# Finishing the last 128 output rows in two column pieces, with two loads and six subtractions on other engines

## The chip, the core and the metric

The kernel runs on one core of a Trainium2 chip. The core has a matmul engine (TensorE, PE in the profile; its weight loads have a row of their own, PEld), and VectorE (DVE), ScalarE (ACT), GpSimd (POOL) and SyncE (SP), which issues most of the DMAs. Each engine works through its own list of instructions in order and waits at semaphores for the others. The metric is the time of one execution on the device in microseconds; less is better. The runs of the kernel before took 843.01, 843.52 and 845.77 us, median 843.52.

## The reference

One inference step of a two-layer trunk for a prompt of 512 rows and a sample group of 8 x 4 = 32 rows, all in float32, width 1024. The first layer is a pooling mixer with memory attention; the second is multi-head latent attention (8 heads, rotary part of 64, a paged cache of 4096 positions for the sample group) with memory attention. What the change touches is the end of the second layer:

```
# second layer
mixed = concat([tok * silu(gate_t), mem_o * silu(gate_m)], -1)   # 1536 wide
x = x + mixed @ w_out[l]                                          # 1536 x 1024
...
# the end: for each row
y = x * rsqrt(mean(x * x) + 1e-6) * g_final
```

and, in the attention, the tables of the rotary part:

```
rope(x) = concat([x1 * cos - x2 * sin, x1 * sin + x2 * cos])
```

## The kernel before, in words

Matmuls run on numbers that are split in two: `split` (lines 88 to 91) makes a high part by a cast on ScalarE and a low part by a subtraction on VectorE or GpSimd, and `mm3` (lines 93 to 96) issues three matmuls, high by high, high by low and low by high, into the same sum. So each weight tile costs a load, a cast, a subtraction, and each product three matmuls.

The program goes through the first layer, the second layer's projections and its memory attention, and then comes to a stretch in which the order on PE and on SP is written out by the program itself (`manual_schedule`, lines 918 to 921). There, `weave` (line 933) takes generators, each a thread of work (`round_scores`, `round_values` for the sample group's cache pages, `gates_late`, `head_inputs`, `heads` for the prompt's attention, `out_all` for the output product, `sample_out` for the sample rows' end), and always lets the one that is furthest behind issue its next piece; a generator yields the time that its piece is planned to take and the time until its next piece may start. The order on ScalarE, VectorE and GpSimd, including the DMAs that GpSimd issues, is chosen by the framework's scheduler from a simulated timeline.

The places that matter here:

- Lines 1138 to 1149: the pools of the heads' stage take over the space of the projections' weights; the two rotary tables, `tab`, are loaded there by SP, 128 x 512 numbers each (256 KB), ahead of the rest of the cache pages that SP loads (line 985). GpSimd issues the loads of the heads' weights (`load_q`, `load_pair`, lines 1151 to 1164). `rope_T` (lines 739 to 749), with GpSimd as its engine, is the tables' reader. The `tab` buffers are used again for two parts of the product's input (`mix_b`, line 1308).
- `prepare` (line 1329): for one slab of the output weights (two blocks of 128 rows by 512 columns, 512 KB) it loads it by SP (`slab`, line 1322), casts the high part on ScalarE and has GpSimd subtract the low part. There are six slabs for each of two column halves, `fh` 0 and 1, so twelve; three buffers each. For the first half it also splits the parts of the product's input that the slab needs (`mix_b`).
- `out_rows` (line 1356): the product for one column half, as four blocks `j` of 128 rows by 512 columns, each in one accumulation bank of the tag "oa". For slab after slab, each block gets 2 x 3 matmuls; the slabs 4 and 5 are done together at the end (the list `late`), so that a block's last 12 matmuls stand together and it is finished before the next block's begin.
- `done` (line 1366): the end of a block. VectorE adds the residual (line 1369), ScalarE squares and sums along the row (line 1370). In the second half, VectorE adds the two halves' sums (line 1375), `rstd_cols` (line 153) has VectorE divide by the width and add the epsilon (line 155) and GpSimd take the power of -0.5 (line 159), ScalarE scales the first column half (line 1379), VectorE scales the second and multiplies it by the gain (line 1381), and SP stores each half (lines 1380 and 1382).
- `sample_out` (line 1558): the sample rows' output product, its two sums in banks of the tag "ac" (line 1570), of which there are two (line 959).

Of the kernel before, what the change touches and what calls it, by code (L numbers as in the profile page):

```python
# [8 lines left out]
F32R = mybir.dt.float32r  # L9
U32 = mybir.dt.uint32  # L10
I32 = mybir.dt.int32
AF = mybir.ActivationFunctionType
ALU = mybir.AluOpType
AX = mybir.AxisListType

P = 128
D = 1024
KD = 8
SEQ = 512
# [5 lines left out]
EPS = 1e-6  # L25
# [13 lines left out]
def trunk_kernel(ctx: ExitStack, tc: tile.TileContext, A, O):  # L39
    nc = tc.nc  # L40
# [35 lines left out]
    def fr(ap):  # L76
        return ap.bitcast(F32)
# [10 lines left out]
    def split(h, l, src, eng=None):  # L88
        nc.scalar.copy(h, src)  # L89
        (eng or nc.vector).tensor_tensor(out=l, in0=src, in1=fr(h), op=ALU.subtract)  # L90
        return h, l

    def mm3(out, wh, wl, xh, xl, start, stop):
        nc.tensor.matmul(out, lhsT=wh, rhs=xh, start=start, stop=False)  # L94
        nc.tensor.matmul(out, lhsT=wh, rhs=xl, start=False, stop=False)  # L95
        nc.tensor.matmul(out, lhsT=wl, rhs=xh, start=False, stop=stop)  # L96
# [16 lines left out]
    ps_ = Banks(pa=4, tr=3, ac=1)  # L113

    def cst(shape, dt=F32):
        return const.tile(shape, dt, name=nm("c"))

    def st(n):
        return small("s", n=n)
# [11 lines left out]
    mhalf = cst([P, 16])  # L131
# [18 lines left out]
    def gain(base, k):  # L150
        return gT[:, base + k : base + k + 1]

    def rstd_cols(ssq, n, rows, width, r=None):
        v = st(n)
        nc.vector.tensor_scalar(
            out=v[:rows], in0=ssq[:rows], scalar1=1.0 / width, scalar2=EPS, op0=ALU.mult, op1=ALU.add
        )
        r = st(n) if r is None else r
        nc.gpsimd.tensor_tensor(out=r[:rows], in0=v[:rows], in1=mhalf[:rows, :n], op=ALU.pow)
        return r  # L160
# [45 lines left out]
    def load_w(src, k, c):  # L206
        t = pw("wr")
        v = t[:, : k * c].rearrange("p (k c) -> p k c", k=k)
        nc.sync.dma_start(v, src)
        return t, v  # L210

    def split_w(t, k, c, eng=None):
        n = k * c
        h, l = split(pw("wh", F32R, n), pw("wl", F32R, n), t[:, :n], eng)
        return h.rearrange("p (k c) -> p k c", k=k), l.rearrange("p (k c) -> p k c", k=k)
# [289 lines left out]
    for k in range(KD):  # L505
        for i in range(2):
            wh, wl = (t.rearrange("p (k c) -> p k c", k=KD) for t in fw[i])
            for half in range(2):
                o = half * HALF
                h, l = hx[k]  # L510
# [10 lines left out]
    t, v = load_w(wa[22], KD, P)  # L521
    wh, wl = split_w(t, KD, P)
# [118 lines left out]
    for f in range(KD):  # L641
        pts = [ps_("pa"), ps_("pa")]
        for s in range(2):
            t = pw("wr")
            nc.sync.dma_start(t[:, :768], wo[f, s].rearrange("p k c -> p (k c)"))
            wh, wl = split_w(t, 6, P, nc.gpsimd)
            for half in range(2):
                o = half * HALF
                for i, k in enumerate(order[s * 6 : s * 6 + 6]):
                    h, l = mixed[k]  # L650
# [26 lines left out]
    for f in (2, 0, 1):  # L677
        c = P if f < 2 else 64
        t, v = load_w(wkv[:, f * P : f * P + c].rearrange("(k p) c -> p k c", p=P), KD, c)
        if f < 2:  # L680
            wh, wl = split_w(t, KD, c)
# [28 lines left out]
    for j in range(4):  # L710
        t = xo("o")
        for k0 in range(0, KD, 4):
            ps = ps_("tr")
# [5 lines left out]
    ps = ps_("tr")  # L719
# [14 lines left out]
    for f in range(2):  # L734
        nc.vector.scalar_tensor_tensor(
            out=ck[f], in0=ck[f], scalar=gain(G_CKV, f), in1=rc, op0=ALU.mult, op1=ALU.mult
# [15 lines left out]
    tab = [rp("c"), rp("c")]  # L752
# [7 lines left out]
    ps = ps_("tr")  # L760
# [201 lines left out]
    def ps_(tag):  # L962
        return (rb if tag in rb.tags else hb)(tag)
# [180 lines left out]
    def pat(tag, dt=F32, n=None):  # L1144
        return next(p for p in (heads_raw, heads_val, heads_in) if tag in p.tags)(tag, dt, n)

    tab = [pat("tab"), pat("tab")]
    nc.sync.dma_start(tab[0], A["c_cos"][:, :SEQ])
    nc.sync.dma_start(tab[1], A["c_sin"][:, :SEQ])

    def load_pair(n):
        t = pat("wu")
# [152 lines left out]
    fin = Pool("fin", "left", wr=(D, 3), wh=(D, 3), wl=(D, 3))  # L1305
    mixed = {}

    def mix_b(k):
        if k >= 8:
            t = pat("tab")  # L1310
            nc.gpsimd.dma_start(t, gmd[k - 8])
            mixed[k] = split(pc("c", F32R), pat("p", F32R), t)
        else:
            mixed[k] = split(pc("c", F32R), (pg("g", F32R) if k else pt("t", F32R))[:, :SEQ], gt[k][:, :SEQ])

    wo = A["w_out_b"]
    ssq = st(8)
    sss = st(2)
    slabs = [(fh, s) for fh in range(2) for s in range(6)]
    order = ([0, 1], [2, 3], [4, 5], [8, 9], [10, 11], [6, 7])  # L1320
# [1 line left out]
    def slab(t, fh, s):  # L1322
        k = order[s][0]
        v = t.rearrange("p (k c) -> p k c", k=2)
        src = wo[k * P : (k + 2) * P, fh * 512 : (fh + 1) * 512]
        nc.sync.dma_start(v, src.rearrange("(k p) c -> p k c", p=P))
        return v

    def prepare(fh, s):
        if fh == 0:  # L1330
            for k in order[s]:
                mix_b(k)
        t = fin("wr")
        slab(t, fh, s)
        wh, wl = split(fin("wh", F32R), fin("wl", F32R), t, nc.gpsimd)
        return wh.rearrange("p (k c) -> p k c", k=2), wl.rearrange("p (k c) -> p k c", k=2)

    prepared = [prepare(*slabs.pop(0)) for _ in range(3)]
    x1n, gains_f = [], []

# [14 lines left out]

    def out_rows(fh):
        pts = [ps_("oa") for _ in range(4)]
        pts = [pts[j] for j in (0, 3, 1, 2)]

        def run(s, j, wh, wl):  # L1360
            c = slice(j * P, (j + 1) * P)
            for i, k in enumerate(order[s]):
                h, l = mixed[k]
                mm3(pts[j], h[:, c], l[:, c], wh[:, i, :], wl[:, i, :], s == 0 and i == 0, s == 5 and i == 1)

        def done(j):
            f = slice(fh * 512, (fh + 1) * 512)
            xf = x1n[j][:, f]
            nc.vector.tensor_tensor(out=xf, in0=pts[j], in1=xf, op=ALU.add)
            nc.scalar.activation(pat("wu"), xf, AF.Square, accum_out=ssq[:, 2 * j + fh : 2 * j + fh + 1])  # L1370
            if fh == 0:
                nc.vector.tensor_tensor(out=xf, in0=xf, in1=gains_f[0][:, f], op=ALU.mult)
                return
            sq = st(1)
            nc.vector.tensor_tensor(
                out=sq, in0=ssq[:, 2 * j : 2 * j + 1], in1=ssq[:, 2 * j + 1 : 2 * j + 2], op=ALU.add
            )
            r = rstd_cols(sq, 1, P, D)
            nc.scalar.activation(x1n[j][:, :512], x1n[j][:, :512], AF.Copy, scale=r)
            nc.sync.dma_start(O["y_p"][0, j * P : (j + 1) * P, :512], x1n[j][:, :512])  # L1380
            nc.vector.scalar_tensor_tensor(out=xf, in0=xf, scalar=r, in1=gains_f[0][:, f], op0=ALU.mult, op1=ALU.mult)
            nc.sync.dma_start(O["y_p"][0, j * P : (j + 1) * P, 512:], xf)

        late = []
        for s in range(6):
            wh, wl = prepared.pop(0)
            late.append((s, wh, wl))
            if s == 4:
                continue
            for j in range(4):  # L1390
                for one in late:
                    run(one[0], j, *one[1:])
                    yield 1.4, 0.0
                if s == 5:
                    if not x1n:
                        yield lambda: x1n
                    done(j)
            for _ in late:
                if slabs:
                    prepared.append(prepare(*slabs.pop(0)))  # L1400
            late = []

    def out_all():
        yield from out_rows(0)
        yield from out_rows(1)
# [35 lines left out]
    out = Thread(out_all(), 112 / total, 66 / total, 66.0, now[0])  # L1441
# [293 lines left out]
```

## Time and profile before

| what | us |
|---|---|
| runs: median (lowest, highest) | 843.52 (843.01, 845.77) |
| the profiled execution's own time | 836.92 |
| its span in the profile | 835.2 |
| PE busy in the span | 792.8 |
| VectorE, ScalarE, GpSimd busy | 506.1, 326.9, 262.4 |

The page of the profile gives the busy time of each engine, the span in forty slices, the DMA queues, the chain of work that ended last, and the costliest groups of instructions. A row of a group names the line, the engine, the operation, the tile written and the tiles read, their shapes and the count; then the busy time in microseconds, the mean of one in nanoseconds, and the idle time of the engine just before such instructions with what ended it. A row of the timeline begins with the start and the duration in microseconds; a bracket at its end is the idle time before it and the releaser. A row of a window gives its length and then the busy time and count of PE, PEld, DVE, ACT and POOL, the granted clock of PE, the DMA share and GB/s. In the list of waits each row says who waited for whom, the total, how often, and the longest. A wait is put down to what came last by the profile. Matmuls are pipelined: a row's duration runs into the next one's, so the distance between starts is what a matmul costs in a stream.

The profiled execution was 836.92 us long, 6.60 us under the median of the runs; 1.7 us of it lie around the span.

### The profile page before, as it was taken

The numbers are of one execution on the slowest core, as the hardware profiler recorded it, in microseconds if no ns is written. First come the engines' busy times: TensorE is split into PE (matmuls) and PEld (weight loads), VectorE is DVE, ScalarE is ACT, GpSimd is POOL, SyncE is SP. The second block draws the span as 40 slices with busy tenths as digits, with TensorE's granted clock in tenths as the row PEclk, the third lists the DMA queues.
The fourth block names the chain that finished last, engine by engine and source line by source line (L and its number), as shares of the span: only waits on it lengthen the run. The fifth ranks groups of instructions, "written<-read, shape, count | busy, mean of one in ns | idle before, by whom it ended". The sixth has DMA issues, their size and how long they took to land.

```text
span 835.2 us, 17542 instructions
## 1 busy us (share of the span) xinstructions
PE 792.8 (95%) x6906; PEld 680.8 (82%) x6906; DVE 506.1 (61%) x941; ACT 326.9 (39%) x650; POOL 262.4 (31%) x213
## 2 busy tenths in 40 slices
PE   6999999978999999999999999899999999999995
PEld 6989998978999989877999897776767767677674
DVE  6757666888763435775766653665665577643313
ACT  7453333322343226335433323444543545342212
POOL 0035223434334313411522342642250230055321
PEclk9999999999999999999999999999999999999999
DMA  8356246511233234636625785967978767776642
GB/s 302 98 179 225 76 177 228 158 58 52 68 121 96 77 120 150 206 89 221 227 89 183 260 295 181 366 225 239 300 246 279 262 205 247 261 267 236 215 177 107
DMA packets 82100, 158.01 MB, mean 189 GB/s; under 512 B 9185, under 2 KB 34402, under 8 KB 81762
## 3 DMA queue, kind: packets, MB, share of 16 engines
q1 hardware_dynamic: 77170, 141.22, 50.9%
q0 software_dynamic: 4848, 15.67, 5.2%
q8 instruction: 54, 0.88, 0.4%
q14 instruction: 28, 0.23, 0.1%
HBM read 147.23 MB, written 9.64 MB: 188 GB/s over the span
## 4 chain that ended last, share of the span: by engine, by line
PE 73%; DVE 10%; DMA 8%; issue 3%; ACT 3%; POOL 2%; SPq 1%; POOLq 0%; DVEq 0%; ACTq 0%
PE pa L94 14%; PE pa L96 14%; PE pa L95 14%; PE tr L135 5%; PE ac L1028 3%; PE ac L1067 3%; DVE v L583 2%; DMA o<-ostore 2%; PE oa L94 2%; PE oa L95 2%; DMA b<-in_cache_P 2%; PE oa L96 2%; PE ac L1039 1%; PE ac L389 1%; SPq L985 1%
## 5 line engine op out<-in xcount | busy, mean ns | idle before, releaser
L94 PE MATMUL pa<-h,wh 128*128 128x272 f32 x832 | 239.7, 291 | 4.5 <-DVE g L613 4.5
L96 PE MATMUL pa<-h,wl 128*128 128x272 f32 x832 | 236.9, 290 | 0.6 <-POOL wl L90 0.6
L90 POOL TENSOR_TENSOR wl<-wr,wh 128x1024 fp32r<-128x1024 f32 (+1 forms) x67 | 156.0, 2330 | 234.7 <-ACT wh L89 220.6
L95 PE MATMUL pa<-h,wh 128*128 128x272 f32 x640 | 184.3, 289 | 0.0
L94 PEld LDWEIGHTS pa<-h,wh 128*128 128x128 f32 x832 | 156.9, 189 | 9.3 <-issue 5.8
L96 PEld LDWEIGHTS pa<-h,wl 128*128 128x128 f32 x832 | 155.6, 189 | 2.4 <-POOL wl L90 1.5
L89 ACT CAST wh<-wr 128x1024 fp32r<-128x1024 f32 (+1 forms) x87 | 87.7, 1008 | 168.4 <-issue 66.8
L95 PEld LDWEIGHTS pa<-h,wh 128*128 128x128 f32 x640 | 120.9, 189 | 1.0
L261 DVE SCALAR_TENSOR_TENSOR g<-t,g 128x272 f32<-128x272 f32 x48 | 49.5, 1037 | 15.3 <-ACT t L260 15.3
L95 PE MATMUL pa<-g,wh 128*128 128x272 f32 x192 | 54.5, 288 | 0.1
L260 ACT ACTIVATE t<-g 128x272 f32<-128x272 f32 x48 | 20.3, 428 | 78.6 <-DVE g L247 78.0
L135 PE MATMUL tr<-c,b 128*128 128x128 f32 x256 | 40.0, 277 | 3.0 <-DVE kt L996 1.7
L94 PE MATMUL oa<-wh,c 128*128 128x512 f32 x96 | 39.5, 412 | 0.0
L95 PE MATMUL oa<-wl,c 128*128 128x512 f32 x96 | 38.0, 395 | 0.7 <-POOL wl L90 0.7
L135 PEld LDWEIGHTS tr<-c,b 128*128 128x128 f32 x256 | 29.7, 140 | 9.7 <-issue 3.0
L95 PEld LDWEIGHTS pa<-g,wh 128*128 128x128 f32 x192 | 36.1, 188 | 0.3 <-DVE g L90 0.3
L994 ACT COPY kt<-tr 128x512 f32<-128x512 f32 x43 | 25.3, 589 | 27.0 <-PE tr L135 26.0
L247 DVE SCALAR_TENSOR_TENSOR g<-pa,r 128x272 f32<-128x272 f32 x42 | 18.2, 438 | 28.8 <-PE pa L96 28.8
L1028 PE MATMUL ac<-kt,c 128*32 128x256 f32 x256 | 35.0, 393 | 0.0
L1028 PE MATMUL ac<-a,c 128*32 128x256 f32 x256 | 34.7, 392 | 0.0
L90 DVE TENSOR_TENSOR q<-q,q 128x512 fp32r<-128x512 f32 x16 | 27.2, 1700 | 10.0 <-ACT q L89 9.9
L90 DVE TENSOR_TENSOR wl<-wr,wh 128x1024 fp32r<-128x1024 f32 x20 | 24.5, 1224 | 12.3 <-ACT wh L89 12.2
(380 smaller groups left out, 1813.0 us busy)
## 6 DMA issues: line engine op xcount, KB each, us to landing
a<-in_cache_P SPq DMA_DIRECT2D x128, 288.0 KB, 4.7
b<-in_cache_P SPq DMA_DIRECT2D x128, 160.0 KB, 4.9
wr<-in_w_in_a SPq DMA_DIRECT2D x24, 512.0 KB, 3.6
wr<-in_w_in_b SPq DMA_DIRECT2D x19, 512.0 KB, 3.6
cs<-in_mem_kT SPq DMA_DIRECT2D x16, 512.0 KB, 5.7
wr<-in_w_out_a SPq DMA_DIRECT2D x16, 384.0 KB, 3.1
wr<-in_w_out_b SPq DMA_DIRECT2D x12, 512.0 KB, 6.3
ws<-in_w_out_b SPq DMA_DIRECT2D x12, 512.0 KB, 5.6
```

Of the source, the lines that this page charges most:

```text
L89: nc.scalar.copy(h, src)
L90: (eng or nc.vector).tensor_tensor(out=l, in0=src, in1=fr(h), op=ALU.subtract)
L94: nc.tensor.matmul(out, lhsT=wh, rhs=xh, start=start, stop=False)
L95: nc.tensor.matmul(out, lhsT=wh, rhs=xl, start=False, stop=False)
L96: nc.tensor.matmul(out, lhsT=wl, rhs=xh, start=False, stop=stop)
L135: nc.tensor.transpose(out, in_, ident[:k, :k])
L247: nc.vector.scalar_tensor_tensor(out=out[:, o : o + HALF], in0=ps[:, :HALF], scalar=scale, in1=bc[:, o : o + HALF], op0=ALU.mult, op1=ALU. ...
L260: nc.scalar.activation(th[:, :HALF], z[:, o : o + HALF], AF.Tanh)
L261: nc.vector.scalar_tensor_tensor(out=z[:, o : o + HALF], in0=th[:, :HALF], scalar=1.0, in1=z[:, o : o + HALF], op0=ALU.add, op1=ALU.mult,)
L994: nc.scalar.copy(out, src)
L1028: nc.tensor.matmul(o[j * NS : (j + 1) * NS, :], lhsT=QT[:, k, b, :], rhs=(nat[ih][0][:, :, PGW + k * P : PGW + (k + 1) * P] if j < 2 else ...
L1067: nc.tensor.matmul(po[j * NS : (j + 1) * NS, :256], lhsT=pT[:, i * P + j * NS : i * P + (j + 1) * NS], rhs=nat[i // 2][j // 2][:, j % 2 * ...
```

## The change

Three edits. The two rotary tables are loaded by GpSimd's queue instead of SP's. The six slabs of the first column half have their low part subtracted by VectorE, those of the second half by GpSimd as before. And in the second column half the last block (block 3, rows 384 to 511) is summed in two pieces of 256 columns, the first in its "oa" bank, the second in an "ac" bank; each is added to the residual and squared by itself. The row sum is put together otherwise for all blocks: the square takes the factor 1024^-0.5 with it, so the sum is a mean already; the epsilon and the sums that are known earlier are added ahead, and behind the last square stand one addition on VectorE and the power on GpSimd.

```
-    nc.sync.dma_start(tab[0], A["c_cos"][:, :SEQ])
-    nc.sync.dma_start(tab[1], A["c_sin"][:, :SEQ])
+    nc.gpsimd.dma_start(tab[0], A["c_cos"][:, :SEQ])
+    nc.gpsimd.dma_start(tab[1], A["c_sin"][:, :SEQ])
...
-    ssq = st(8)
+    ssq = st(16)
...
-        wh, wl = split(fin("wh", F32R), fin("wl", F32R), t, nc.gpsimd)
+        wh, wl = split(fin("wh", F32R), fin("wl", F32R), t, nc.vector if fh == 0 else nc.gpsimd)
...
+        pieces = [[(pts[j], 0, 512)] for j in (0, 3, 1, 2)]
+        if fh:
+            pieces[3] = [(pts[2], 0, 256), (ps_("ac"), 256, 256)]
+
+        def run(s, j, piece, wh, wl):
+            ps, o, n = piece
+            c, w = slice(j * P, (j + 1) * P), slice(o, o + n)
             for i, k in enumerate(order[s]):
                 h, l = mixed[k]
-                mm3(pts[j], h[:, c], l[:, c], wh[:, i, :], wl[:, i, :], s == 0 and i == 0, s == 5 and i == 1)
+                mm3(ps[:, :n], h[:, c], l[:, c], wh[:, i, w], wl[:, i, w], s == 0 and i == 0, s == 5 and i == 1)
+        def done(j, p, ps, o, n):
+            f = slice(fh * 512 + o, fh * 512 + o + n)
             xf = x1n[j][:, f]
-            nc.vector.tensor_tensor(out=xf, in0=pts[j], in1=xf, op=ALU.add)
-            nc.scalar.activation(pat("wu"), xf, AF.Square, accum_out=ssq[:, 2 * j + fh : 2 * j + fh + 1])
+            nc.vector.tensor_tensor(out=xf, in0=ps[:, :n], in1=xf, op=ALU.add)
+            c = 4 * j + 2 * fh + p
+            nc.scalar.activation(pat("wu", n=n), xf, AF.Square, scale=D ** -0.5, accum_out=ssq[:, c : c + 1])
...
+            if p < len(pieces[j]) - 1:
+                return
+            others = [4 * j] + [4 * j + 2 + i for i in range(p)]
+            so_far = EPS
+            for i, o_ in enumerate(others):
+                nc.vector.tensor_scalar(
+                    out=sm[:, i : i + 1], in0=ssq[:, o_ : o_ + 1], scalar1=so_far, scalar2=None, op0=ALU.add
+                )
+                so_far = sm[:, i : i + 1]
+            r = st(1)
+            nc.vector.tensor_scalar(
+                out=sm[:, 2:3], in0=ssq[:, c : c + 1], scalar1=so_far, scalar2=None, op0=ALU.add
             )
-            r = rstd_cols(sq, 1, P, D)
+            nc.gpsimd.tensor_tensor(out=r, in0=sm[:, 2:3], in1=mhalf[:, :1], op=ALU.pow)
             nc.scalar.activation(x1n[j][:, :512], x1n[j][:, :512], AF.Copy, scale=r)
...
             for j in range(4):
-                for one in late:
-                    run(one[0], j, *one[1:])
-                    yield 1.4, 0.0
+                for p, piece in enumerate(pieces[j]):
+                    for one in late:
+                        run(one[0], j, piece, *one[1:])
+                        yield 1.4 / len(pieces[j]), 0.0
```

More of the change, by code (lines that the diff above doesn't have):

```diff
@@ L1357, in out_rows @@
         pts = [ps_("oa") for _ in range(4)]
-        pts = [pts[j] for j in (0, 3, 1, 2)]
-        def run(s, j, wh, wl):
-            c = slice(j * P, (j + 1) * P)
+        pieces = [[(pts[j], 0, 512)] for j in (0, 3, 1, 2)]
[4 more added lines that the diff above has]
+            c, w = slice(j * P, (j + 1) * P), slice(o, o + n)
             for i, k in enumerate(order[s]):
                 h, l = mixed[k]
-                mm3(pts[j], h[:, c], l[:, c], wh[:, i, :], wl[:, i, :], s == 0 and i == 0, s == 5 and i == 1)
-        def done(j):
-            f = slice(fh * 512, (fh + 1) * 512)
+                mm3(ps[:, :n], h[:, c], l[:, c], wh[:, i, w], wl[:, i, w], s == 0 and i == 0, s == 5 and i == 1)
+        def done(j, p, ps, o, n):
+            f = slice(fh * 512 + o, fh * 512 + o + n)
             xf = x1n[j][:, f]
-            nc.vector.tensor_tensor(out=xf, in0=pts[j], in1=xf, op=ALU.add)
-            nc.scalar.activation(pat("wu"), xf, AF.Square, accum_out=ssq[:, 2 * j + fh : 2 * j + fh + 1])
+            nc.vector.tensor_tensor(out=xf, in0=ps[:, :n], in1=xf, op=ALU.add)
+            c = 4 * j + 2 * fh + p
+            nc.scalar.activation(pat("wu", n=n), xf, AF.Square, scale=D ** -0.5, accum_out=ssq[:, c : c + 1])
             if fh == 0:
@@ L1373, in done @@
                 return
-            sq = st(1)
-            nc.vector.tensor_tensor(
-                out=sq, in0=ssq[:, 2 * j : 2 * j + 1], in1=ssq[:, 2 * j + 1 : 2 * j + 2], op=ALU.add
+            sm = st(3)
+            if p < len(pieces[j]) - 1:
[10 more added lines that the diff above has]
+                out=sm[:, 2:3], in0=ssq[:, c : c + 1], scalar1=so_far, scalar2=None, op0=ALU.add
             )
-            r = rstd_cols(sq, 1, P, D)
+            nc.gpsimd.tensor_tensor(out=r, in0=sm[:, 2:3], in1=mhalf[:, :1], op=ALU.pow)
             nc.scalar.activation(x1n[j][:, :512], x1n[j][:, :512], AF.Copy, scale=r)
             nc.sync.dma_start(O["y_p"][0, j * P : (j + 1) * P, :512], x1n[j][:, :512])
-            nc.vector.scalar_tensor_tensor(out=xf, in0=xf, scalar=r, in1=gains_f[0][:, f], op0=ALU.mult, op1=ALU.mult)
+            xf = x1n[j][:, 512:]
+            nc.vector.scalar_tensor_tensor(out=xf, in0=xf, scalar=r, in1=gains_f[0][:, 512:], op0=ALU.mult, op1=ALU.mult)
             nc.sync.dma_start(O["y_p"][0, j * P : (j + 1) * P, 512:], xf)
@@ L1390, in out_rows @@
             for j in range(4):
-                for one in late:
-                    run(one[0], j, *one[1:])
-                    yield 1.4, 0.0
[L1394 to L1397, printed above, removed]
+                for p, piece in enumerate(pieces[j]):
+                    for one in late:
+                        run(one[0], j, piece, *one[1:])
+                        yield 1.4 / len(pieces[j]), 0.0
+                    if s == 5:
+                        if not x1n:
+                            yield lambda: x1n
+                        done(j, p, *piece)
             for _ in late:
```

## The prediction

> **What bounds the kernel now.** I read the page first, then who waited for whom on the matmul engine in the last stage, then that stage in order of time.
>
> ```profile
> span 835.2 us, 17542 instructions
> PE 792.8 (95%) x6906; PEld 680.8 (82%) x6906; DVE 506.1 (61%) x941; ACT 326.9 (39%) x650; POOL 262.4 (31%) x213
> ```
> ```profile
> PE tr L1509 <- DMA o<-ostore: 1.1, 1, 1.1
> PE tr L135 <- ACT rt L1050: 1.1, 1, 1.1
> PE oa L95 <- POOL wl L90: 0.7, 1, 0.7
> PE ac L1575 <- DMA ws<-in_w_out_b: 0.4, 1, 0.4
> ```
> ```profile
> 505.00:724.00 219.00, 208.86 (x2248) 156.85 (x2247) 138.88 (x314) 100.93 (x240) 63.51 (x65) 1.00 0.76 251
> ```
> The matmul engine (PE) works 95% of the span. From 724 us on it waits only four times, 3.3 us together (second fence, the window from 724 to 836 us), and one of the four, 0.7 us, is for a low part made by GpSimd: this is what the second part of the change touches. The third fence is one long window in the attention stage before it, its length and then PE's busy time; I come back to it under C. The last matmul ends at 826.54 us (its row stands below), and 8.7 us pass from there to the end of the span: this tail is what the first part of the change touches. So there are two places with something to win, and both are small.
>
> **The first weights' low parts.** This is the spot where PE goes from the last head to the output product.
>
> ```profile
> 736.49 1.05 ACT L89 CAST wh<-wr 128x1024 fp32r<-128x1024 f32 x1 [0.85 <-DMA wr<-in_w_out_b]
> 737.66 0.27 ACT L89 CAST p<-hs 128x128 fp32r<-128x128 f32 x1
> 737.82 1.05 ACT L89 CAST wh<-wr 128x1024 fp32r<-128x1024 f32 x1
> ```
> ```profile
> 737.67 5.18 POOL L90 TENSOR_TENSOR wl<-wr,wh 128x1024 fp32r<-128x1024 f32 x2 [14.57 <-ACT wh L89]
> ```
> ```profile
> 737.96 0.29 DVE L90 TENSOR_TENSOR p<-hs,p 128x128 fp32r<-128x128 f32 x1 [3.87 <-ACT p L89]
> 738.17 0.68 DVE L996 COPY kt<-tr 128x512 f32<-128x512 f32 x1
> 738.76 4.64 DVE L90 TENSOR_TENSOR p<-tab,c 128x512 fp32r<-128x512 f32 x2
> ```
> ```profile
> 738.86 0.28 PE L102 MATMUL po<-p,vx 128*128 128x128 f32 x1
> 738.97 0.45 PE L94 MATMUL oa<-wh,c 128*128 128x512 f32 x1
> 740.10 0.50 PE L95 MATMUL oa<-wl,c 128*128 128x512 f32 x1 [0.68 <-POOL wl L90]
> ```
> ```profile
> L90 DVE TENSOR_TENSOR wl<-wr,wh 128x1024 fp32r<-128x1024 f32 x20 | 24.5, 1224 | 12.3 <-ACT wh L89 12.2
> L90 DVE TENSOR_TENSOR g<-g,c 128x512 fp32r<-128x512 f32 x7 | 4.8, 686 | 0.2
> ```
> ScalarE casts the first slab's high part until 737.54; GpSimd then takes until about 740.1 for the low part, and PE, which started its first output matmul at 738.97 and could have gone on some 0.23 us later, starts the second at 740.10. The same subtraction on VectorE takes 1.22 us elsewhere in this run (mean of 20). VectorE is idle for 3.87 us up to 737.96, so it can take it. Two orders are likely on its queue. Low part of the slab first: done at 738.8, the last head's 128x128 low part behind it at 739.1, so L102 moves from 738.86 to about 739.16, and L95 starts at about 739.5. The head's part first: it ends at 738.25, the slab's at 739.5, and L95 starts then too. Both give 740.10 - 739.5 = 0.60 us. If the copy of 0.68 us goes ahead as well, the slab's low part ends at 740.1 and nothing is won. I take -0.60, with ends 0 and -0.9 (L95 straight behind L94, 740.10 - 739.20).
>
> The other five low parts have more time, since PE takes 24 matmuls for each slab; at 1.22 us each VectorE has 6.1 us more to do over some 25 us. GpSimd's work of some 2.5 us each goes away, and with it what stretched VectorE: two subtractions of 128x512 took 4.64 us beside GpSimd's, where the same form costs 0.686 us as a mean of seven. I count on 1.22 us for the six because nothing of this kind is then left for GpSimd there; were it still running, the ratio of those rows (2.32 to 0.686) would make 4.1 us of 1.22, and the first low part would end 1.6 us later than it does now. [...]
>
> Whether an advance of 0.6 us at 740 reaches the end: the next waits of PE hang on PE's own progress. The load of ostore that PE waits for is queued on SP behind loads whose buffers are freed when the last sample attention matmul has read them, so it moves along; the late slab load of 0.4 us also starts when PE frees its buffer. I keep -0.60.
>
> **The tail.**
>
> ```profile
> 826.58 0.69 DVE L1369 TENSOR_TENSOR x<-oa,x 128x512 f32<-128x512 f32 x1 [0.89 <-PE oa L96]
> 827.19 0.74 DVE L1381 SCALAR_TENSOR_TENSOR x<-x,s,g 128x512 f32<-128x512 f32 x1
> 828.12 0.16 DVE L1375 TENSOR_TENSOR s<-s 128x1 f32<-128x1 f32 x1 [0.19 <-ACT wu L1370]
> 828.31 0.15 DVE L155 TENSOR_SCALAR s<-s 128x1 f32<-128x1 f32 x1
> 829.13 0.75 DVE L1381 SCALAR_TENSOR_TENSOR x<-x,s,g 128x512 f32<-128x512 f32 x1 [0.67 <-POOL s L159]
> ```
> ```profile
> 827.36 0.63 ACT L1370 ACTIVATE wu<-x 128x512 f32<-128x512 f32 x1 [0.29 <-DVE x L1369]
> 827.90 0.19 ACT L1370 ACTIVATION_READ_ACCUMULATOR wu<-x 128x1 f32 x1
> ```
> ```profile
> L90 DVE TENSOR_TENSOR p<-hs,p 128x256 fp32r<-128x256 f32 x8 | 3.4, 423 | 4.1 <-ACT p L89 3.9
> ```
> ```profile
> 801.25 0.31 ACT L1588 ACTIVATE wu<-c 128x128 f32<-128x128 f32 x1 [2.93 <-DVE c L1587]
> 801.46 0.19 ACT L1588 ACTIVATION_READ_ACCUMULATOR wu<-c 128x1 f32 x1
> ```
> ```profile
> 590.17 0.28 PE L95 MATMUL pa<-wul,c 128*128 128x256 f32 x1
> ```
> ```profile
> 591.35 0.28 PE L96 MATMUL pa<-wuh,c 128*128 128x256 f32 x1
> ```
> ```profile
> 818.00 0.40 PE L94 MATMUL oa<-wh,c 128*128 128x512 f32 x1
> ```
> ```profile
> 826.14 0.40 PE L96 MATMUL oa<-wh,g 128*128 128x512 f32 x1
> ```
> What stands between the last matmul and the end is a chain of residual add, square with its sum, two small VectorE steps, the power on GpSimd, and the scaling of both halves. Step by step:
>
> The add handles 256 columns: 0.423 us by the row from PSUM, for 0.69: -0.27. The square's sum is read 0.54 us behind its start for 512 columns and 0.21 us for 128 (both pairs of rows); in proportion 0.32 for 256: -0.22, with ends 0 and -0.33. The two small steps become one, because the epsilon and the earlier sums are added ahead: 828.31 - 828.12, so -0.19, with ends 0 and -0.19. The ahead-of-time adds (0.15 each by the L155 row) lie under the 0.54 us of the square; without that cover they cost what they save. The division by the width rides on the square as its scale and adds no instruction. The power, both scalings and both stores stay as they are.
>
> Against that stands the cost on PE: the 36 matmuls of the last block become 72. Ten steps from 590.17 to 591.35 give 0.118 us for 256 columns with a weight load each; 35 steps from 818.00 to 826.14 give 0.2326 for 512. 72 x 0.118 - 36 x 0.2326 = +0.12 us. The first piece is added and squared while the second runs (12 x 0.118 = 1.4 us), so it lies beside. The multiplication of the third block (827.19, 0.74) stands behind the last add on VectorE; were it in front, the add would start later: up to +0.4. Sum of the tail: -0.27 - 0.22 - 0.19 + 0.12 = -0.56, ends -0.8 and +0.1.
>
> The second piece holds one of the two "ac" banks from the first slab of the second half to the end, so the two sample output sums share the other:
>
> ```profile
> 800.86 0.29 DVE L1587 TENSOR_TENSOR c<-ac,c 128x128 f32<-128x128 f32 x1 [6.76 <-PE ac L1575]
> ```
> ```profile
> 802.31 0.64 PE L1575 MATMUL ac<-ws,c 128*32 128x128 f32 x16
> ```
> The second sum starts at 802.31 and must then wait for the add of the first, which is over at 801.15, 1.2 us early: nothing.
>
> **The tables.**
>
> ```profile
> 503.68 0.70 SPq L1149 DMA_DIRECT2D tab<-in_c_sin  x1
> 516.99 1.91 SPq L985 DMA_DIRECT2D a<-in_cache_P  x4
> ```
> ```profile
> 516.08 2.05 POOL L90 TENSOR_TENSOR ql<-qw,qh 128x384 fp32r<-128x384 f32 x2 [15.50 <-ACT qh L89]
> ```
> ```profile
> 522.77 1.39 POOL L747 TENSOR_TENSOR t<-t,tab 128x512 f32<-128x512 f32 x1 [0.32 <-DVE c L1091]
> ```
> ```profile
> L1311 POOL DMA_DIRECT2D tab<-gmd x4: 544/562/585, 670.3 to 743.7; - x4
> ```
> On SP the two loads (the second is shown) stand where SP has nothing else until 516.99, so taking them away frees nobody. On GpSimd two loads of this size cost 2 x 0.56 = 1.1 us, behind which the loads of the first head weights queue and then the subtraction of 516.08; before that GpSimd is idle 15.50 us, which hides them. Without that cover they would be issued by 516.08 + 2.05 + 1.1 = 519.2, 3.5 us before their first use at 522.77, and the rotation would wait for what a landing takes beyond that. I take 0.
>
> **Sum.** -0.60 - 0.56 = -1.16 us on the profiled execution's 836.92 (span 835.2 and 1.7 around it): 835.76. The median of the runs, 843.52, lies 6.60 above the profiled one; I carry the difference over: 842.4 us.
>
> **The rivals.**
> A. VectorE's queue puts more than one slab ahead of the last head's low part (slower). ScalarE's cast for the second slab ends at 738.87, one straight behind it for the third would end at 739.92. With two slabs ahead of it the head's part ends at 738.87 + 1.22 + 0.29 = 740.4, and L95 starts at about 740.8, +0.7; with three ahead at 739.92 + 1.22 + 0.29 + 0.4 = 741.8, +1.7, and with the copy of 0.68 as well +2.4. It turns to a loss from the second slab on. The largest, with the tail: 843.52 - 0.56 + 2.4 = 845.4. Against it: ScalarE casts the head's part (737.66) ahead of the second slab's.
> B. A weight load costs time of its own. The 128-column matmuls (738.86 to 738.97) follow at 0.11 us, so a load needs about that much; if it were not covered, 36 more loads cost 36 x 0.11 = +4.0, and 843.52 - 0.60 - 0.68 + 4.0 = 846.2. [...] The rows speak against it: 0.118 with a load at each step leaves no room.
> C. The order on ScalarE, VectorE and GpSimd is drawn up anew by the scheduler when an engine changes. From 505 to 724 us PE is idle 219 - 208.86 = 10.1 us in small handoffs; a quarter more or less is 2.5 us: 840 or 845, and beyond where the measurement adds its spread.
> D. Nothing is won: the copy goes ahead of the first slab, and the third block's multiplication ahead of the last add: 843.52 - 0.1 = 843.4.
>
> **How the numbers follow.** Forecast 0.55, A 0.10, B 0.03, C 0.17 (half each way), D 0.15. A measurement can tell about 0.3% here, 2.5 us (the runs themselves lie between 843.01 and 845.77), so the forecast and D count as no change. Faster by more needs C's good half and some of the forecast's upper end: 0.14. Slower by more: C's bad half, B and the end of A: 0.13. The range 840.0 to 845.6 takes in both halves of C and A's end, and leaves out B and the rest of C's ends.
>
> **What would show it.** Right: no wait of PE for a low part at 740; the four waits down to three; VectorE's six slab steps at about 1.2 us; 72 matmuls of 256 columns at 0.12 us; from the end of the last matmul to the power's end about 1.9 us instead of 2.56. Wrong: a PE wait for a head's low part or for VectorE near 739; steps above 0.13 us; a wait for the tables at 522; a new order between 505 and 724 that moves PE's start at 739 by more than the tail's gain.

## The result and the profile after

The changed kernel took 851.07 us (median of 20 runs, 846.27 to 857.45) beside 839.85 us of the kernel before (20 runs, 836.04 to 846.37; the three runs known at the prediction lay in the upper part of that). The ratio is 1.0123, with a 95% interval of 1.0102 to 1.0144: slower by 1.2%, some 10 us. The forecast was 842.4 us, no change, with a range of 840.0 to 845.6; 851.07 lies well above it. The profiled execution took 850.78 us against 836.92 of the one before, 13.9 us more; a single execution is no median, but it shows the places.

The span is 848.9 us, for 835.2. First the changed kernel's row for the attention stage, whose counterpart the prediction showed (length; busy time of PE, PEld, VectorE, ScalarE, GpSimd; granted clock, DMA share, GB/s):

```profile
505.00:724.00 219.00, 203.77 (x2154) 153.38 (x2152) 135.85 (x293) 98.76 (x233) 62.44 (x64) 0.98 0.74 246
```
PE's busy time in these 219 us fell from 208.86 to 203.77 us: 5.1 us more idle, in a stage in which the change touches only where two tables are loaded. The list of waits of PE after, from 505 to 730 us and then from 730 us on (line numbers after the edits are 17 higher at the end: L1526 was L1509, L1592 was L1575):

```profile
PE pa L94 <- DVE q L1206: 5.9, 3, 4.9
```
```profile
PE tr L1526 <- DMA o<-ostore: 2.8, 1, 2.8
PE ac L1592 <- DMA ws<-in_w_out_b: 1.9, 1, 1.9
PE tr L135 <- ACT rt L1050: 1.1, 1, 1.1
PE po L102 <- DVE p L90: 0.3, 1, 0.3
```
Three things are seen. A wait for the scaled q (`pa L94`) has one case of 4.9 us. Of the four waits of the last stage one has gone, that for GpSimd's low part, as forecast; a smaller one for the head's low part, 0.3 us, came. And the two waits that nobody meant to touch, for ostore and for the sample's output weights `ws`, went from 1.1 and 0.4 to 2.8 and 1.9 us.

**The first rotation.** The timelines of VectorE, GpSimd and PE where the long wait is, in the changed kernel:

```profile
523.45 0.69 DVE L1206 SCALAR_TENSOR_TENSOR t<-pa,r 128x512 f32<-128x512 f32 x1 [0.42 <-PE pa L96]
524.17 2.79 DVE L745 COPY t<-t 32x512 f32<-32x512 f32 x2
527.00 0.16 DVE L1091 TENSOR_TENSOR c<-s,s 128x1 f32<-128x1 f32 x1
527.08 1.44 DVE L1093 TENSOR_SCALAR os<-os,s 128x256 f32<-128x256 f32 x1
528.44 2.90 DVE L1092 SCALAR_TENSOR_TENSOR c<-s,s,c 128x1 f32<-128x1 f32 x1
531.26 0.68 DVE L1206 SCALAR_TENSOR_TENSOR q<-pa,r 128x512 f32<-128x512 f32 x1
```
```profile
527.11 1.26 POOL L746 TENSOR_TENSOR t<-t,tab 128x512 f32<-128x512 f32 x1 [0.42 <-issue]
528.32 0.76 POOL L1154 DMA_DIRECT2D wu<-in_w_v_up  x1
529.10 1.00 POOL L90 TENSOR_TENSOR ql<-qw,qh 128x384 fp32r<-128x384 f32 x1
530.04 1.26 POOL L748 TENSOR_TENSOR t<-t,t 128x512 f32<-128x512 f32 x1
```
```profile
531.99 0.79 PE L94 MATMUL pa<-c,wuh 128*128 128x512 f32 x1 [4.94 <-DVE q L1206]
```
The same stretch of VectorE in the kernel before:

```profile
521.99 0.68 DVE L1206 SCALAR_TENSOR_TENSOR t<-pa,r 128x512 f32<-128x512 f32 x1
522.59 0.15 DVE L1091 TENSOR_TENSOR c<-s,s 128x1 f32<-128x1 f32 x1
522.66 0.35 DVE L1093 TENSOR_SCALAR os<-os,s 128x256 f32<-128x256 f32 x1
523.02 2.07 DVE L745 COPY t<-t 32x512 f32<-32x512 f32 x2
525.12 0.22 DVE L1092 SCALAR_TENSOR_TENSOR c<-s,s,c 128x1 f32<-128x1 f32 x1
525.26 0.68 DVE L1206 SCALAR_TENSOR_TENSOR q<-pa,r 128x512 f32<-128x512 f32 x1
```
The same six rows stand there in another order: the rotation's two row copies (L745) now go ahead of L1091 and L1093. From the first L1206 to the second it was 3.27 us and is 7.81. Two rows carry most of the difference, 3.77 of 4.54 us: L1093 takes 1.44 us for 0.35, and L1092, a step on one number per row, 2.90 us for 0.22; the two copies add 0.72. L1092 ends at 531.34, and GpSimd's L748 at 531.30. PE waits 4.94 us where it waited 0.41.

A second cost comes behind that wait. Windows of 4 us after (PE's busy time behind the length; the granted clock is the third number from the end):

```profile
528.00:532.00 4.00, 0.01 (x1) 0.01 (x1) 4.00 (x4) 0.03 (x1) 3.29 (x4) 0.78 1.06 388
532.00:536.00 4.00, 4.00 (x14) 2.88 (x18) 1.42 (x3) 1.59 (x3) 0.00 (x0) 0.50 0.27 93
536.00:540.00 4.00, 4.00 (x47) 2.72 (x40) 1.58 (x3) 1.09 (x2) 2.06 (x3) 0.87 0.42 119
```
When PE is back at work, its clock is 0.50 for 4 us and 0.87 for the next four: 0.50 x 4 + 0.13 x 4 = 2.5 us of work lost on top of the wait. In the kernel before, the clock of these twelve microseconds was 1.00.

**The last stage.** The rows at the first slab after, VectorE and then PE:

```profile
747.20 1.23 DVE L90 TENSOR_TENSOR wl<-wr,wh 128x1024 fp32r<-128x1024 f32 x1 [3.74 <-ACT wh L89]
748.34 0.28 DVE L90 TENSOR_TENSOR p<-hs,p 128x128 fp32r<-128x128 f32 x1
```
```profile
748.68 0.33 PE L102 MATMUL po<-p,vx 128*128 128x128 f32 x1 [0.30 <-DVE p L90]
748.84 0.45 PE L94 MATMUL oa<-wh,c 128*128 128x512 f32 x1
749.13 0.40 PE L95 MATMUL oa<-wl,c 128*128 128x512 f32 x1
```
L95 starts 0.29 us behind L94; before it was 1.13. Part of this gain is paid back one step ahead, where L102 waits 0.30 us for the head's low part: the distance of PE's rows to those before falls from 9.36 us ahead of the spot (L102 at 747.49 for 738.13) to 8.92 behind it (the second L94 at 749.59 for 740.67), a net gain of 0.44 us. The six low parts together, by the groups of the last stage:

```profile
L90 DVE TENSOR_TENSOR wl<-wr,wh 128x1024 fp32r<-128x1024 f32 x6 | 7.3, 1221 | 6.0 <-ACT wh L89 6.0
```
This part went as forecast, with the slab's subtraction ahead of the head's on VectorE, the first of the two orders that the prediction named. What follows did not. The rows of SP's queue, first before, then after:

```profile
757.91 6.62 SPq L1326 DMA_DIRECT2D ws<-in_w_out_b  x5
764.76 0.37 SPq L1562 DMA_DIRECT2D o<-ostore  x1
765.23 20.54 SPq L1326 DMA_DIRECT2D wr<-in_w_out_b  x4
```
```profile
770.73 3.92 SPq L1326 DMA_DIRECT2D ws<-in_w_out_b  x5
774.90 2.74 SPq L1579 DMA_DIRECT2D o<-ostore  x1
779.87 13.25 SPq L1326 DMA_DIRECT2D wr<-in_w_out_b  x3
```
Four slab loads (`wr`) stood behind ostore, now three: one went ahead of the five `ws` loads, and ostore is issued 10.1 us later than before (774.90 - 764.76), while PE's matmuls for the slabs stand only 8.9 us later (an L94 at 757.97 for 749.06, another at 787.40 for 778.48). So the load falls behind PE, and PE's wait for it grows by 1.7 us, from 1.09 to 2.78. Behind that wait the clock falls again:

```profile
792.00:796.00 4.00, 4.00 (x30) 2.35 (x23) 2.41 (x5) 0.72 (x2) 0.73 (x1) 0.63 0.72 252
796.00:800.00 4.00, 4.00 (x21) 3.32 (x21) 2.17 (x7) 0.00 (x0) 0.00 (x0) 0.94 0.02 8
```
That is (0.37 + 0.06) x 4 = 1.7 us of work, where the kernel before has a clock of 1.00 at the same place (from 780 to 804 us).

**The tail**, from the last matmul on, after:

```profile
840.03 0.28 PE L96 MATMUL ac<-wh,g 128*128 128x256 f32 x1
...
840.14 0.75 DVE L1397 SCALAR_TENSOR_TENSOR x<-x,s,g 128x512 f32<-128x512 f32 x1
840.81 0.42 DVE L1373 TENSOR_TENSOR x<-ac,x 128x256 f32<-128x256 f32 x1
...
841.87 0.21 DVE L1390 TENSOR_SCALAR s<-s,s 128x1 f32<-128x1 f32 x1 [0.64 <-ACT wu L1375]
842.16 0.55 POOL L1393 TENSOR_TENSOR s<-s,c 128x1 f32<-128x1 f32 x1 [2.05 <-DVE s L1390]
```
From the end of the last matmul (840.31) to the power's end (842.71) it is 2.40 us; it was 2.56, and 1.9 was forecast. The add starts 0.50 us behind the last matmul, not at once, because the third block's multiplication (L1397) stands ahead of it on VectorE.

The 13.9 us of the profiled pair stand as follows, by the distance of equal rows before and after. By 509 us, ahead of every edit, 1.65 us (nothing changed there, so this is one execution against another). Across the first rotation 6.7, to 692 us 1.0 more, at the first slab -0.4, at the transposition that waits for ostore +1.7, from there to the last matmul +3.3, in the tail -0.2. The 3.3 are the longer wait for `ws` (1.88 for 0.42 us, so 1.5) and the 1.7 us of clock just shown. The 6.7 are the longer wait for the scaled q (4.94 for 0.41, so 4.5) and most of the 2.5 us of clock behind it.

### The profile page after: what moved, and what is told of

Its sections match the earlier page's. It is cut to its first block, busy times and chain, and to the rows that moved or that the text cites. A ratio compares the mean times of both kernels' runs of the same rounds, so it can differ in the third digit from the quotient of the medians.

```text
span 848.9 us, 17618 instructions
## 1 busy us (share of the span) xinstructions
PE 797.9 (94%) x6942; PEld 686.8 (81%) x6942; DVE 509.8 (60%) x949; ACT 327.0 (39%) x652; POOL 247.3 (29%) x209
## 4 chain that ended last, share of the span: by engine, by line
PE 70%; DVE 10%; DMA 9%; issue 6%; ACT 3%; POOL 1%; SPq 1%; POOLq 0%; DVEq 0%; ACTq 0%
PE pa L94 14%; PE pa L96 14%; PE pa L95 14%; PE tr L135 5%; PE ac L1067 3%; PE ac L1028 3%; DVE v L583 2%; DMA o<-ostore 2%; PE ac L1039 1%; PE oa L94 1%; DMA b<-in_cache_P 1%; PE oa L96 1%; PE oa L95 1%; PE ac L389 1%; DMA wr<-in_w_mem_v 1%
## 5 line engine op out<-in xcount | busy, mean ns | idle before, releaser
L94 PE MATMUL pa<-h,wh 128*128 128x272 f32 x832 | 240.4, 291 | 4.5 <-DVE g L613 4.5
L90 POOL TENSOR_TENSOR wl<-wr,wh 128x1024 fp32r<-128x1024 f32 (+1 forms) x61 | 140.0, 2296 | 219.7 <-ACT wh L89 206.2
L95 PE MATMUL pa<-h,wh 128*128 128x272 f32 x640 | 184.8, 290 | 0.0
L94 PEld LDWEIGHTS pa<-h,wh 128*128 128x128 f32 x832 | 157.5, 190 | 9.3 <-issue 5.8
L95 PEld LDWEIGHTS pa<-h,wh 128*128 128x128 f32 x640 | 121.5, 190 | 1.0
L95 PE MATMUL pa<-g,wh 128*128 128x272 f32 x192 | 54.5, 288 | 0.1
L90 DVE TENSOR_TENSOR wl<-wr,wh 128x1024 fp32r<-128x1024 f32 x26 | 31.8, 1224 | 18.2 <-ACT wh L89 18.1
L94 PE MATMUL oa<-wh,c 128*128 128x512 f32 (+1 forms) x96 | 38.6, 402 | 0.0
L95 PE MATMUL oa<-wl,c 128*128 128x512 f32 (+1 forms) x96 | 37.0, 385 | 0.0
L95 PEld LDWEIGHTS pa<-g,wh 128*128 128x128 f32 x192 | 36.1, 188 | 0.3 <-DVE g L90 0.3
```

## The experiments

Two theories were set against each other first: that the tables' new place is the larger part (T), and that the new place of a slab load on SP is (S). Ratios are to the kernel before on the same chip, with the 95% interval; each kernel had 12 runs, the kernel before 35 in each of three rounds (medians 839.75, 840.42 and 840.89 us).

| run | what it is | ratio (interval) |
|---|---|---|
| e1_tables | only the tables | 1.0069 (1.0041 to 1.0097) |
| e2_lows | only the six low parts | 1.0006 (0.9980 to 1.0032) |
| e3_tail | only the pieces and the shorter sum | 1.0027 (0.9999 to 1.0056) |
| e4_no_tables | the change without the tables | 1.0039 (1.0010 to 1.0068) |
| e5_tables_scalar | tables on ScalarE's queue | 1.0004 (0.9979 to 1.0029) |
| e6_cos_gpsimd | one table on GpSimd's queue | 1.0024 (1.0000 to 1.0048) |
| e12_copies | tables on GpSimd, row copies on ScalarE | 0.9985 (0.9962 to 1.0008) |
| e11_copies_alone | row copies on ScalarE | 0.9966 (0.9936 to 0.9995) |
| e8_five_lows | five low parts | 0.9984 (0.9969 to 0.9998) |
| e10_tail_one_place | pieces issued together | 0.9989 (0.9968 to 1.0010) |
| e13_five_lows_tail | five low parts, pieces together | 0.9963 (0.9943 to 0.9984) |
| e15_with_copies | the same and the row copies | 0.9956 (0.9935 to 0.9976) |

**The three parts alone.** e1_tables:

```
-    nc.sync.dma_start(tab[0], A["c_cos"][:, :SEQ])
-    nc.sync.dma_start(tab[1], A["c_sin"][:, :SEQ])
+    nc.gpsimd.dma_start(tab[0], A["c_cos"][:, :SEQ])
+    nc.gpsimd.dma_start(tab[1], A["c_sin"][:, :SEQ])
```


> Only the two table loads move to GpSimd's queue; low parts and tail stay as before. Theory T (the tables' place on GpSimd's queue draws up a new order of small steps at the first rotation, where VectorE and GpSimd then stretch each other, and this is the larger part of the loss): slower than before by 5 to 8.5 us, with PE's wait for the turned q at L94 near 4.9 us instead of 0.4 and its third copy (L1206) over 6 us later. Theory S (the loss comes from the last stage, where the slab load now stands ahead of five ws loads on SP): no change, within 1.5 us, and the last stage as before. Theory K (nothing but a lower granted clock in some executions): no change in the median.

It took 845.31 us against 839.75, a ratio of 1.0069, and its wait is that of the changed kernel:

```profile
530.87 0.80 PE L94 MATMUL pa<-c,wuh 128*128 128x512 f32 x1 [4.94 <-DVE q L1206]
```
The tables alone bring 0.7 of the 1.2%. Theory T holds for the larger part, and S can't be all.

e2_lows:

```
-        wh, wl = split(fin("wh", F32R), fin("wl", F32R), t, nc.gpsimd)
+        wh, wl = split(fin("wh", F32R), fin("wl", F32R), t, nc.vector if fh == 0 else nc.gpsimd)
```


> Only the six low parts of the first half's weight slabs move from GpSimd to VectorE. Theory S (VectorE frees the slab's buffer sooner, so the ninth slab load goes ahead of five ws loads and of ostore on SP, and PE waits for ostore and for ws): slower than before by 2 to 5 us, PE's waits for ostore and ws together near 4.7 us instead of 1.5; the place at 740 gains 0.6. Theory T (all of the loss is the tables): faster by 0.6 us or no change. Forecast of the prediction for this part alone: -0.6 us.

840.90 against 839.75, ratio 1.0006: no change, neither the gain of 0.6 us nor a loss of 2. The mechanism of S is in its trace all the same, the slab load ahead of ostore and a longer wait:

```profile
781.77 1.08 PE L1509 MATMUL tr<-o,t 128*32 128x256 f32 x8 [2.94 <-DMA o<-ostore]
```
```profile
784.00:788.00 4.00, 4.00 (x21) 2.00 (x14) 2.05 (x4) 0.68 (x2) 0.00 (x0) 0.50 0.44 146
```
Behind it the clock falls to 0.50 again (second fence, the window from 784 to 788 us). So S exists, but as a size it was too high.

e3_tail has the third part of the diff, `out_rows` as in the changed kernel, and nothing else of it.

> Only the last block in two column pieces with the shorter sum. Theories T and S alike, and the prediction: -0.5 us (between -0.8 and +0.1), 0.1 us more on PE and some 0.66 us less between the last matmul and the power's end. A rival that puts the loss of the last stage on the held ac bank or on the 36 added weight loads: slower by 3 to 5 us, with a PE wait for an ac bank, or 256-column steps above 0.13 us.

841.39 against 839.75, ratio 1.0027, which the interval hardly parts from none; the expectation of -0.5 us failed, and the rival's 3 to 5 is not reached either. The 256-column steps are 0.118 us, and no ac bank is waited for, so the rival's causes are out. What grew is another wait; the row after, and the one before:

```profile
806.99 0.64 PE L1592 MATMUL ac<-ws,c 128*32 128x128 f32 x16 [1.81 <-DMA ws<-in_w_out_b]
```
```profile
803.38 0.64 PE L1575 MATMUL ac<-ws,c 128*32 128x128 f32 x16 [0.42 <-DMA ws<-in_w_out_b]
```
The window behind that wait in e3_tail has the fallen clock:

```profile
808.00:812.00 4.00, 4.00 (x39) 2.69 (x38) 0.00 (x0) 0.00 (x0) 0.16 (x1) 0.57 0.76 284
```
PE reaches this matmul earlier in its work. Behind the wait stood 84 block matmuls of 512 columns before; now 72 and 48 of 256 columns are left, as much as 96: twelve matmuls, 12 x 0.2326 = 2.8 us of work, have moved from ahead of the wait to behind it. The edit yields between the two pieces, and the loop that weaves the threads puts sample matmuls into that gap.

e4_no_tables is the changed kernel with the tables back on SP.

> The changed kernel with the two table loads back on SP; low parts on VectorE and the pieces stay. Theory T: faster than the changed kernel by 5 to 8.5 us, PE's wait for the turned q back to about 0.4 us, the time between before - 1 and before + 5. Theory S alone: still slower than before by all of the 11 us. If the two causes add: before + 2 to + 5 us, with PE's waits for ostore and ws near 4.7 us.

843.00 against 839.75, ratio 1.0039: 3.3 us over before, as "the two causes add" had it. PE's wait for q is 0.5 us at most again, those for ostore and ws are 1.9 and 2.0. The three parts alone sum to 0.0069 + 0.0006 + 0.0027 = 0.0102, the lower end of the whole's interval.

**Why the tables cost.** GpSimd's queue isn't what delays: ahead of its first step behind the two issues GpSimd still sits idle for 15.51 us, 15.50 before, and what ends this is ScalarE's cast of qh. The step starts 1.06 us later than the 1.65 us account for (518.79 for 516.08), because that cast has moved: before, ScalarE makes it between two copies of kt, now behind both. With one table on GpSimd (e6_cos_gpsimd, below) the cast stays between them, and the idle time is 15.00 us, shorter by one issue. What changed is the order of other instructions, so the next runs change the order and the queue apart. e5_tables_scalar:

```
+    nc.scalar.dma_start(tab[0], A["c_cos"][:, :SEQ])
+    nc.scalar.dma_start(tab[1], A["c_sin"][:, :SEQ])
```


> The kernel before with the two table loads on ScalarE's queue: SP loses them as in the change, but the order of all other instructions on VectorE, GpSimd and ScalarE stays that of before. Theory O (the loss is the new order of small steps that the scheduler draws up when GpSimd has two loads more): same as before, within 1.5 us, PE's wait for the turned q at L94 0.4 us. Rival Q (the loss comes from taking the tables off SP, or from when their transfers land): slower by about 5.8 us, as with the tables on GpSimd.

840.47 against 840.42, ratio 1.0004, PE's wait 0.39 us, and VectorE's six rows stand in the order of before. Taking the tables off SP costs nothing that these runs can tell; Q falls.

e6_cos_gpsimd moves only the first of the two loads to GpSimd's queue.

> The kernel before with one of the two tables on GpSimd's queue. GpSimd's order changes as with both (the load of the next value weights and one low part change places between the three steps of the rotation), ScalarE's casts too; VectorE's order is that of before, its two row copies (L745) stay behind L1091 and L1093. Theory D (VectorE's two copies ahead of those steps cost the time): same as before, PE's wait at L94 near 0.4 to 1 us. Theory P (GpSimd's order, which puts its steps beside other VectorE steps and stretches them): slower by 4 to 6 us, PE's wait near 4.9 us.

842.29 against 840.42, ratio 1.0024, between the two theories. PE's wait for q is 0.35 us (527.85), as D has it, so GpSimd's order alone does not make the long wait. But it has a cost of its own, one step later; VectorE and PE:

```profile
528.47 4.19 DVE L90 TENSOR_TENSOR q<-q,q 128x512 fp32r<-128x512 f32 x1
```
```profile
533.92 0.39 PE L94 MATMUL pa<-wuh,c 128*128 128x256 f32 x1 [1.52 <-DVE kx L90]
```
The subtraction of q, 1.40 us in the kernel before, takes 4.19 and ends at 532.66, 0.56 us behind the end of a run of three GpSimd steps (528.90 to 532.10), as if it had waited for all three.

e12_copies has both tables on GpSimd, and this:

```
-            nc.vector.tensor_copy(sw[r + 32 : r + 64, :n], x[r : r + 32, :n])
+            (nc.scalar.copy if eng is nc.gpsimd else nc.vector.tensor_copy)(sw[r + 32 : r + 64, :n], x[r : r + 32, :n])
```


> Both tables on GpSimd's queue, and the rotation's two row copies (L745) on ScalarE instead of VectorE. GpSimd's new order stays, but VectorE has no copies left to put ahead of L1091, L1093 and L1092. Theory D (those two copies, taking 2.8 us beside GpSimd's steps, push the turned q behind a run of GpSimd steps): PE's wait at L94 back from 4.9 to 0.4 to 1.5 us, no dip of the clock at 530, the time 1 to 3 us over the same kernel with the tables on SP. Theory P (GpSimd's order alone): as slow as the tables alone, about 5.8 us over before, with the wait of 4.9.

839.15 against 840.89, ratio 0.9985. The loss of 0.7% is gone although the tables stay on GpSimd and GpSimd's steps stand in the new order. VectorE and PE:

```profile
524.33 1.21 DVE L1091 TENSOR_TENSOR c<-s,s 128x1 f32<-128x1 f32 x1
526.84 0.21 DVE L1092 SCALAR_TENSOR_TENSOR c<-s,s,c 128x1 f32<-128x1 f32 x1
526.97 0.68 DVE L1206 SCALAR_TENSOR_TENSOR q<-pa,r 128x512 f32<-128x512 f32 x1
```
```profile
527.71 0.51 PE L94 MATMUL pa<-c,wuh 128*128 128x512 f32 x1 [0.38 <-DVE q L1206]
```
L1092 is at 0.21 us again, and it now runs ahead of GpSimd's L746 (from 527.03 in this run), not beside it. Theory D is shown for the long wait: it is there with VectorE's two copies ahead of those small steps (e1_tables), and it is gone with the copies behind L1091 and L1093 (e6_cos_gpsimd) and with no copies there (here). In time the evidence is thinner, because moving the copies gains something by itself (next run). That GpSimd's steps are what stretches L1092 is read from the rows alone: 531.34 against 531.30 us for the ends after, e6_cos_gpsimd's subtraction, and L1091 in this run, which takes 1.21 us for 0.15 and ends at 525.54, where a GpSimd subtraction ends at 525.51. It wasn't tried by itself, and the rows do not show how the one engine holds up the other: L1092's 2.90 us span the issue of a DMA and two steps of GpSimd (528.32 to 531.30).

e11_copies_alone has that edit on the kernel before.

> The kernel before with the rotation's row copies on ScalarE, tables on SP: what the copies' move does by itself, for the comparison with the run that has the tables on GpSimd. VectorE's two copies took 2.07 us at the first rotation, in front of the turned q that PE waited 0.4 us for; ScalarE's two more are 1.25 us. Expected: no change, within 1.5 us.

837.73 against 840.89, ratio 0.9966 (0.9936 to 0.9995): a little faster, where no change was expected; a miss, with an interval that nearly reaches 1. Between it and e12_copies, 0.9985, the intervals overlap: with the copies away, the tables' place costs 0.2% by the two ratios, which these runs cannot tell from nothing, where it costs 0.7% with the copies on VectorE.

**Why the other two parts gave nothing.** e8_five_lows:

```
+        wh, wl = split(fin("wh", F32R), fin("wl", F32R), t, nc.vector if fh == 0 and s < 5 else nc.gpsimd)
```


> The kernel before with five of the six low parts of the first half on VectorE; the sixth stays on GpSimd, and with it the ninth slab load stays behind the ws loads and ostore on SP. Theory S (the low parts' gain of 0.6 us is eaten by that slab load ahead of ostore): PE's wait for ostore back from 2.9 to about 1.1 us, no dip of the clock at 780, 0.6 us faster than before or, with the dip, 2 us faster than with all six. Rival (the moved low parts load VectorE itself): no difference to all six, with ostore's wait still above 2 us.

839.17 against 840.42, ratio 0.9984 (0.9969 to 0.9998). The slab load is behind ostore again, and the wait is shorter:

```profile
783.47 0.64 PE L1509 MATMUL tr<-o,t 128*32 128x256 f32 x8 [1.53 <-DMA o<-ostore]
```
This is the way S goes, 0.22% better than all six; but the two intervals overlap, and ostore's wait was 1.0 to 2.0 us in other runs that keep the old order (2.0 in e5_tables_scalar). S is supported, not settled.

e10_tail_one_place, on the kernel before, with the rest of e3_tail:

```
-                        yield 1.4 / len(pieces[j]), 0.0
+                        if p == len(pieces[j]) - 1:
+                            yield 1.4, 0.0
```


> The kernel before with the pieces and the shorter sum, but both pieces of the last block issued together, so that no sample matmuls come between them. Theory F (the loss of the tail alone, 2.3 us, is that the sample's ws matmuls come 1.4 us of other work earlier, wait for their load, and the clock falls behind that wait): PE's wait for ws back to about 0.4 us, no dip of the clock there, 0.5 us faster than before. A rival (the pieces themselves cost it, by weight loads or by the held ac bank): as slow as with the pieces apart, 2 us over before.

840.48 against 840.42, ratio 0.9989 (0.9968 to 1.0010), against 1.0027 with the gap. The wait that grew is back:

```profile
809.93 0.64 PE L1593 MATMUL ac<-ws,c 128*32 128x128 f32 x16 [0.30 <-DMA ws<-in_w_out_b]
```
Behind it stand 60 block matmuls of 512 columns and 48 of 256, as much as the 84 before: the twelve are back ahead of the wait. So the pieces themselves cost nothing that can be told, and F, the gap between them, is what the count and the wait bear out. The times go the same way, but the two intervals still touch (e3_tail's begins at 0.9999, this one ends at 1.0010). The forecast gain of 0.5 us is inside the interval, not shown. The dip of the clock is not bound to this wait alone: this execution has one from 784 to 792 us (a clock of 0.52 and 0.62 in the two windows of 4 us), behind 1.99 us of waiting for ostore.

**What is left when the losses are taken out.** e13_five_lows_tail joins the last two edits, tables on SP.

> What of the change is left when its three losses are taken out: tables on SP, five of the six low parts on VectorE, the last block's two pieces issued together, the shorter sum. If the parts add, 1.3 us for the low parts and 0.9 for the tail, as the two measured alone: about 2.2 us faster than before, between 0.5 and 4.

837.71 against 840.89, ratio 0.9963 (0.9943 to 0.9984): 3.2 us faster than before, inside the expected 0.5 to 4. The gain of 0.0037 is more than the sum of the two alone (0.0027), which lies within its interval. e15_with_copies adds the move of the row copies to ScalarE:

> The same with the rotation's row copies on ScalarE as well. Against the version without: no change, within 1.5 us, since PE waits only 0.4 us for the turned q there.

837.70, ratio 0.9956 (0.9935 to 0.9976), the best of all: 0.4% faster than the kernel before and, by the two ratios, 1.6% faster than the changed kernel (1 - 0.9956 / 1.0123 = 0.0165). Against e13_five_lows_tail it is no change, as expected.

## Why the prediction was wrong

**The tables: the step that failed.** The prediction took 0, because GpSimd's idle time hides the two issues. That time does hide the queue: 15.51 us of it are left, and a cast on ScalarE ends them. But the step priced the queue and left out that the framework's scheduler draws up the order of VectorE, ScalarE and GpSimd from a simulated timeline in which those two issues count. Two loads that no engine waited for moved a cast on ScalarE by one place and two copies on VectorE by two. The prediction had this as rival C, with a chance of 0.17, half of it to the bad side, and priced it as a quarter of PE's idle time from 505 to 724 us, 2.5 us. The idle time grew by half, 10.1 to 15.2 us, and the clock lost another 2.5 us behind it; alone the tables cost 0.7%, 5.6 us. So the term that was put at 0 measured 5.6 us. The mechanism was on the list of rivals, at less than half its size, and the list had no row for the clock.

The rows had a warning: the prediction had itself quoted that VectorE's 0.686 us became 2.32 beside GpSimd, and it used this only for the low parts. The steps ahead of the scaled q, where the tables are first used, take 0.15 + 0.35 + 2.07 + 0.22 = 2.79 us before; by the same ratio, 3.4, they could take up to 6.6 us more. That is an upper estimate (the copies already ran beside GpSimd before); 4.5 us was measured.

**The low parts** went as worked out at their spot: L95 behind L94 by 0.29 us instead of 1.13, six steps of 1.22 us on VectorE (a sum of 7.3), 0.30 us of waiting by L102, no subtraction on GpSimd until 777.46; net 0.44 us on PE, for 0.60. Rival A's queue of several slabs did not form. What failed is the sentence that the load of ostore "moves along": the ninth slab load goes ahead on SP, where the written order has ended, and ostore is later; that VectorE frees the slab's buffer earlier is the likely reason. In the pair this cost 1.7 us at the wait and 1.7 us by the clock. The low parts alone came out at 1.0006, five of them at 0.9984, so the size by itself is not settled.

**The tail.** The price of a piece was right: 0.118 us a step with a weight load at each (6942 matmuls and 6942 loads in the page after), no wait for the ac bank (rival B falls). The third block's multiplication did go ahead of the last add, which was listed as "up to +0.4" and cost 0.46, so that 0.16 of the 0.66 us between the last matmul and the power was won. What the working did not have is the loop's second yield: a place for other threads' work in the middle of a block. It moved the sample's matmuls 2.8 us of work ahead of their loads.

**The sum.** The forecast 842.4 was carried from a median of three runs that lay high. Against the median of 20, 839.85, the same -1.16 us would be 838.7; the error of the mechanism is 12 us, not 8.7: the high base hid a part of it.

## What to carry to other kernels

Where a framework orders some engines by a simulated timeline, a DMA that is moved to another queue is an edit of that order, even if the queue was idle: compare the instruction order of every engine before and after, and price each swap by what runs beside it on GpSimd (here 0.22 us became 2.90). In a loop that weaves threads, a yield is a place where other work goes; splitting a piece adds one, and what comes earlier must have its loads earlier too. And a wait of PE can cost more than its own length: with waits of 4.94 and 2.78 us (after), 2.94 (e2_lows) and 1.81 (e3_tail) went a clock of 0.50 for some 3.4 to 6.9 us, worked out from windows of 4 us, while with one of 2.0 us (e5_tables_scalar) it stayed at 1.00.

## What the runs showed of the hardware

The clock's price was not expected. In the traces of the study the granted clock falls to 0.50 for about 3.4 us or twice that, once three times. In windows of 0.5 us it reads 0.50 from 530.5 to 537.0 after, with 0.75 and 0.93 in the windows at the ends, and from 725.5 to 728.5 in the kernel before, with 0.89 and 0.70. With 0.50 as the level, windows of 4 us give the lengths: (1 - 0.57) x 4 / 0.5 = 3.4 us in e3_tail, (0.22 + 0.50 + 0.13) x 4 / 0.5 = 6.8 us at the first rotation after, (0.20 + 0.50 + 0.50 + 0.08) x 4 / 0.5 = 10.2 us from 724 to 740 us in e8_five_lows. Many of these dips stand where PE stands still or has just stood still: at 4.94 us (the tables alone, and the changed kernel, where the clock falls some 1.7 us before that wait ends at 531.99), behind 2.94 (e2_lows), behind 1.81 (e3_tail). Not every such wait has one: e5_tables_scalar waits 2.0 us for ostore, and its clock there is 1.00. And not every dip has such a wait. The kernel before has one here, with PE busy in all of the 12 us from 716 to 728:

```profile
724.00:728.00 4.00, 4.00 (x53) 2.89 (x56) 1.33 (x7) 0.71 (x3) 0.00 (x0) 0.67 0.97 331
```
The changed kernel has it too, from 735.2 to 738.5 us. So what makes the clock fall stays open; that a long wait brings a dip is an observation.

The clock is a likely reason, not a tried one, why executions of one kernel spread over 10 us (836.04 to 846.37). Of the 35 runs of the kernel before in the last round the fastest, 837.42 us, has a mean granted clock of 0.992 and the slowest, 848.11 us, one of 0.981; 0.011 of 840 us is 9 us, an estimate. The 20 runs of the changed kernel have a median of 0.983, those 35 one of 0.990, so by the same estimate the lower clock goes with some 6 of the 11 us that were lost.

And an instruction on one number per row, 0.22 us long before, took 2.90 us beside GpSimd's steps: its own length did not bound what it cost there.
